# Listing the norms ahead of the merges, and the first weights ahead of the last two operands, in an encoder layer on one core

## The chip, the cores and the metric

The kernel runs on one core of one Trainium2 chip. The metric is device time of one launch, in microseconds (us). The kernel before the change takes 3186.42 us, the median of three runs (3184.72 to 3188.18).

## The reference, cut to what matters

One layer of an encoder is computed for two request groups, a prompt of 512 tokens and a sample of 1024, with the same weights. The model width is 1024, the inner width of the feed-forward block 2816, and all arithmetic is to fp32 accuracy. For a group with rows x:

```
h = rmsnorm(x, norm_pre_mix)
q, k, v, z, xbc, dt, gates = split(h @ w_in)
att = rmsnorm(diff_attention(q, k, v)) @ w_proj_attn
ssm = rmsnorm(ssd_forward + ssd_backward, gated by z) @ w_proj_ssm
merged = sigmoid(gate_att) * att + sigmoid(gate_ssm) * ssm
x  = x + rmsnorm(merged @ w_out, norm_post_mix)
h2 = rmsnorm(x, norm_pre_ffn)
up = h2 @ w_gate_up
y  = x + rmsnorm((silu(up[:, :2816]) * up[:, 2816:]) @ w_down, norm_post_ffn)
```

The change concerns the lines from `merged` to `up`.

## The kernel before, in words

**Tiles and chunks.** The 1536 tokens are worked on as three chunks of 512: chunk 0 is the prompt, chunks 1 and 2 the sample. An fp32 operand is held as a high and a low part in a format that TensorE multiplies (`split`, lines L135 and L136: ScalarE copies the high part, VectorE subtracts it to get the low one; with "act_pool" GpSimd subtracts, L142). A product of two operands is three matmuls per block of 128 rows: high with high (L167), high with low (L168), low with high (L169).

**What sets the order.** The program is written against a tile framework. The Python code lists operations; at compile time a scheduler hands each engine its instructions in one fixed order, in which what is listed first has precedence, and what is listed later fills in where it is ready by the scheduler's own reckoning. Tiles are taken from pools by tags; a tag has a fixed number of slots, and these are handed out in the order of the listing, so that a tile listed later waits for the readers of the one that had its slot before. On the chip every engine goes through its instructions strictly in that order. All loads and stores are issued by SyncE (SP).

**Merge of a chunk** (`merge`, L895 to L914). Four weight panels of 256 columns give eight products of 24 matmuls, each 512 columns wide, into a PSUM tile with the tag "mm", which has six slots. For each product a gate tile is loaded (L905, tag "gt", two slots) and put through tanh on ScalarE (L906), and the part of the state-space branch is loaded (L907, tag "pt", one slot). VectorE then empties the PSUM tile into the gate tile (L910), adds the part (L911), ScalarE writes the high part of the merged block (L912) and VectorE the low one (L913). Merge 0 is done earlier in another way; merge 1 and merge 2 are the ones here.

**Output projection of a chunk** (`out_proj`, L1040). Four panels of `w_out` by four tiles of 128 tokens give 16 PSUM tiles, also with the tag "mm", of 24 matmuls with 256 columns each, 384 matmuls in all. The sum runs over the eight merged blocks, so each of the 16 tiles needs all eight of them. ScalarE copies a PSUM tile to the rows `mt` (L1048) and squares it into a scratch tile of the tag "gt" for the sum of squares (L1050).

**Norms of a chunk** (`norms`, L1053 to L1081). VectorE sums the squares (L1057) and computes the reciprocal root by a short iteration of small instructions (L181 to L186). Then, for eight half rows of 512: the input is loaded (L1065, tag "xr", two slots), the row is scaled (L1066), the input is added (L1067), and ScalarE squares the sum (L1068); a finished row tile is stored (L1069). After a second reciprocal root the four row tiles are scaled (L1074), TensorE transposes them in 32 pieces, four to a PSUM tile (L1078), ScalarE copies each PSUM tile out with the weight of the norm (L1080) into a tile `hr` that takes the tags "gt" and "xr" in turn, and the result is stored for the feed-forward block (L1081).

**Gate-up.** The feed-forward product uses seven products in place of eight on 2 x 2 blocks. The first half of the tokens (768, from chunks 0 and 1) comes first; its operands are built by `Operands`: b11, t2, t3 and t1 by `build_first`, then b21, t4 and b22 by `build`. t4 is computed from b21 and t2; b22 is loaded and split. The sixth and seventh product of each step use t4 and b22. `weights(jb)` (L964) loads the weights of step jb (L974, four loads), forms sums on GpSimd (L989 to L997) and splits the seven results; `gate_up` (L1016) does the seven products of 12 matmuls with 384 columns, and empties them on ScalarE and VectorE (L1021 to L1033). Two steps (NPRE) stand in this part of the program, ahead of the norms of chunk 2; the others follow.

**The listing around the change** is at the end of the code below: the output projection of chunk 0, merge 1, norms of chunk 0, output projection 1, merge 2, norms of chunk 1, the operands, output projection 2, t4, b22, the weights of two steps, the two steps, norms of chunk 2.

Of the kernel before, what the change touches and what calls it, by code (L numbers as in the profile page):

```python
# [41 lines left out]
NPRE = 2  # L42
CB = (1, 1)
RWB = 7
NW = 0
NKEEP = 1
SEQS = ((0, 4), (4, 12))
GROUPS = ((0, 512), (512, 1024))
# [29 lines left out]
def hybrid_trunk_kernel(ctx: ExitStack, tc: tile.TileContext, a: dict, y_prompt, y_sample):  # L78
    nc = tc.nc
    V, S, G, TE = nc.vector, nc.scalar, nc.gpsimd, nc.tensor  # L80
# [3 lines left out]
    def f(ap):  # L84
        return ap.bitcast(F32)
# [273 lines left out]
    with ExitStack() as ph1:  # L359
# [230 lines left out]
        with tc.tile_pool(name="dp", bufs=1, reuse_waits="tile") as dp, tc.tile_pool(name="dp_ps", bufs=2, space=PSUM) as dps:  # L590
# [6 lines left out]
            t1 = dp.tile([P, NT, 32], F32, name="t1")  # L597
# [274 lines left out]
    with ExitStack() as ph3:  # L872
# [22 lines left out]
        def merge(c, aTt):  # L895
            cs = slice(c * 512, (c + 1) * 512)
            hi, lo = big_pair()
            for p0 in range(0, D, 256):
                w = split_panel(a["w_proj_attn"][0][:, p0:p0 + 256])
                for b in range(2):  # L900
                    r0 = p0 + b * P
                    kb = r0 // P
                    gt = wk.tile([P, 512], F32, tag="gt", name="gt")
                    pt = wk.tile([P, 512], F32, tag="pt", name="pt", bufs=1)
                    load(out=gt, in_=g_d[r0:r0 + P, cs])  # L905
                    S.activation(out=gt, in_=gt, func=AF.Tanh, scale=0.5)  # L906
                    load(out=pt, in_=part_d[r0:r0 + P, cs])  # L907
                    ps = mm_tile(512)
                    gemm_fm(ps, w, slice(b * P, (b + 1) * P), aTt)
                    V.scalar_tensor_tensor(gt, gt, 1.0, ps, op0=ALU.add, op1=ALU.mult)  # L910
                    V.tensor_add(gt, gt, pt)  # L911
                    S.activation(out=hi[:, kb, :], in_=gt, func=AF.Copy, scale=0.5)  # L912
                    V.scalar_tensor_tensor(lo[:, kb, :], gt, 0.5, f(hi[:, kb, :]), op0=ALU.mult, op1=ALU.subtract)  # L913
            return hi, lo  # L914
# [101 lines left out]
        def gate_up(t0, jb, ops, w, pool, bufs, tables=True):  # L1016
            c11, c12, c22 = [pool.tile([P, 384], F32, tag=t_, name=t_, bufs=b_)
                             for t_, b_ in (("c11", bufs), ("c12", bufs), ("c22", min(bufs, CB[1])))]
            c21 = wk.tile([P, 384], F32, tag="araw", name="c21", bufs=3) if bufs == 1 else pool.tile(
                [P, 384], F32, tag="c21", name="c21", bufs=CB[0])  # L1020
            S.copy(c11, product(w[0], ops[0]))  # L1021
            V.tensor_add(c12, product(w[1], ops[1]), c11)
            V.tensor_add(c21, product(w[2], ops[2]), c12)
            ps = product(w[3], ops[3])
            V.tensor_add(c22, ps, c21)
            V.tensor_add(c12, ps, c12)
            V.tensor_add(c11, product(w[4], ops[4]), c11)
            V.tensor_add(c21, product(w[5], ops[5]), c21)
            silu_mul(c11, c21, tables)
            store(out=ff_d[t0 // 768][jb * P:(jb + 1) * P, 0:384], in_=c11)  # L1030
            V.tensor_add(c12, product(w[6], ops[6]), c12)
            silu_mul(c12, c22, tables)
            store(out=ff_d[t0 // 768][jb * P:(jb + 1) * P, 384:768], in_=c12)  # L1033

        with ExitStack() as ph3a:
            mp = ph3a.enter_context(tc.tile_pool(name="mp", bufs=1, reuse_waits="tile"))
            pmw = mp.tile([P, D], F32, name="pmw")
            load(out=pmw, in_=a["norm_post_mix"].broadcast_to([P, D]))

            def out_proj(mT):  # L1040
                tiles = [mp.tile([P, D], F32, tag="mt", name="mt", bufs=4) for _ in range(4)]
                sums = wk.tile([P, 4, 4], F32, tag="ms4", name="ms4")
                for p0 in range(0, D, 256):
                    w = split_panel(a["w_out"][0][:, p0:p0 + 256])
                    for j in range(4):
                        ps = mm_tile(256)
                        gemm_tm(ps, w, mT, slice(j * P, (j + 1) * P))
                        S.copy(tiles[j][:, p0:p0 + 256], ps)  # L1048
                        sq = wk.tile([P, 256], F32, tag="gt", name="msq")
                        S.activation(out=sq, in_=ps, func=AF.Square, accum_out=sums[:, j, p0 // 256:p0 // 256 + 1])  # L1050
                return tiles, sums

            def norms(c, arg):  # L1053
                tiles, sums = arg
                v, r, t_ = [wk.tile([P, 2, 4], F32, tag=n, name=n) for n in ("mv", "mr", "mt_")]
                s2 = wk.tile([P, 4, 2], F32, tag="ms2", name="ms2")
                V.reduce_sum(v[:, 0], sums, axis=mybir.AxisListType.X)  # L1057
                V.tensor_scalar(v[:, 0], v[:, 0], 1.0 / D, EPS, op0=ALU.mult, op1=ALU.add)
                rsqrt(r[:, 0], v[:, 0], t_[:, 0])
                for j, mt in enumerate(tiles):  # L1060
                    t = 4 * c + j
                    for o in (0, 512):
                        mo = mt[:, o:o + 512]
                        xt = mp.tile([P, 512], F32, tag="xr", name="xr", bufs=2)
                        load(out=xt, in_=rows(t, a["x_prompt"], a["x_sample"])[:, o:o + 512])  # L1065
                        V.scalar_tensor_tensor(mo, mo, r[:, 0, j:j + 1], pmw[:, o:o + 512], op0=ALU.mult, op1=ALU.mult)  # L1066
                        V.tensor_add(mo, mo, xt)  # L1067
                        S.activation(out=xt, in_=mo, func=AF.Square, accum_out=s2[:, j, o // 512:o // 512 + 1])  # L1068
                    store(out=x2_d[t * P:(t + 1) * P, :], in_=mt)  # L1069
                V.tensor_add(v[:, 1], s2[:, :, 0], s2[:, :, 1])  # L1070
                V.tensor_scalar(v[:, 1], v[:, 1], 1.0 / D, EPS, op0=ALU.mult, op1=ALU.add)
                rsqrt(r[:, 1], v[:, 1], t_[:, 1])
                for j, mt in enumerate(tiles):
                    V.tensor_scalar(mt, mt, r[:, 1, j:j + 1], 0.0, op0=ALU.mult, op1=ALU.add)  # L1074
                for k in range(KB):
                    ps = tr_ps.tile([P, 512], F32, tag="tr", name="tr_ps")
                    for j, xn in enumerate(tiles):
                        TE.transpose(ps[:, j * P:(j + 1) * P], xn[:, k * P:(k + 1) * P], ident)  # L1078
                    hr = (mp if k % 2 else wk).tile([P, 512], F32, tag=("gt", "xr")[k % 2], name="hr", bufs=2)
                    S.activation(out=hr, in_=ps, func=AF.Copy, scale=cols[:, C_FFN + k:C_FFN + k + 1])  # L1080
                    store(out=h2_d[k * P:(k + 1) * P, c * 512:(c + 1) * 512], in_=hr)  # L1081

            def att(c):
                return load_att(c, big_pair(), lambda: [
                    wk.tile([P, 512], F32, tag="araw", name="araw", bufs=3) for _ in range(2)])

            m0 = load_merged(0)
            att_scale(1, zq, msq, ap, tr_ps, "tr")
            aT1 = att(1)
            t0 = out_proj(m0)  # L1090
            m1 = merge(1, aT1)
            norms(0, t0)
            aT2 = att(2)
            t1 = out_proj(m1)
            m2 = merge(2, aT2)
            norms(1, t1)
            ops = Operands(0, wk, "araw", 3)
            ops.build_first()
            ops.build(("b21",), V, "act_dve")
            t2 = out_proj(m2)  # L1100
            ops.build(("t4",), V, "act_dve")
            ops.tag, ops.bufs = OT
            ops.build(("b22",), V, "act_pool")
            w = {jb: weights(jb, "pt", 1) for jb in range(NPRE + NW)}
            for jb in range(NPRE):
                gate_up(0, jb, ops.all(), w[jb], mp, 1, False)
            norms(2, t2)

        with tc.tile_pool(name="fw", bufs=2, reuse_waits="tile") as fw:
            for jb in range(NPRE, FB):  # L1110
                if jb >= NPRE + NW:
                    w[jb] = weights(jb, rpool=fw if jb > NPRE else None)
                gate_up(0, jb, ops.all(), w[jb], fw, 2)
            ops = Operands(768, fw, "rw", RWB)
            ops.build_first()
            ops.build(ops.names[4:], G, "act_dve")
            for jb in reversed(range(FB)):
                if jb < FB - NKEEP:
                    w[jb] = weights(jb, rpool=fw)
                gate_up(768, jb, ops.all(), w[jb], fw, 2)  # L1120
# [104 lines left out]
```

## Time and profile before

| what | value |
|---|---|
| median of three runs | 3186.42 us |
| the profiled execution | 3193.28 us, span of the trace 3191.5 us |
| TensorE (PE) busy | 3035.2 us, 95% of the span |
| VectorE (DVE), ScalarE (ACT), GpSimd (POOL) busy | 57%, 39%, 20% of the span |
| mean granted TensorE clock | 0.98 of full speed |
| merge 1 begins on PE | 1893.17 us after the span's start |
| merge 2 begins | 2004.23 us |
| gate-up begins | 2100.14 us |

A row of a timeline or a group gives engine, line, operation, the tile written and those read, and sizes; what stands in brackets is the idle time of the engine just ahead, and what ended it. PEld is TensorE's loading of weights, which runs beside its matmuls; SPq and the like are an engine's queue of DMA issues. The clock is that which was granted to TensorE.

### The profile page before, as it was taken

What the parts mean: (1) busy time and instruction counts of PE and PEld (TensorE: products, weight loads), DVE (VectorE), ACT (ScalarE), POOL (GpSimd) and SP (SyncE); (2) the same over time, 40 slices, a digit from 0 to 9 for tenths busy, and PEclk for the clock granted to TensorE, in tenths of its full rate; (3) what the DMA queues carried; (4) which work ended last, traced back from release to release, by engine and by line L of the source; (5) the groups of instructions that cost most, each with busy time, mean ns of one, the idle gap of its engine ahead of it and who ended that gap; (6) DMA issues with size and microseconds to landing.
All of it is one profiled execution on the core that took longest, in us unless ns stands there. A gap on an engine that the chain in (4) does not pass through costs nothing. (4 is left out here: it accounts for less than half of the span.)

```text
span 3191.5 us, 44134 instructions
## 1 busy us (share of the span) xinstructions
PE 3035.2 (95%) x16667; PEld 2672.3 (84%) x16667; DVE 1826.8 (57%) x2957; ACT 1260.0 (39%) x2305; POOL 650.7 (20%) x508
## 2 busy tenths in 40 slices
PE   7999999999999999899999898978999999989998
PEld 7988887888787777788877787878999899978887
DVE  5214444455327996387778845676666766632444
ACT  4103333333303333366666645543333333332443
POOL 0001111000133442243232100023333433300000
PEclk9999999999999999999999999989999999999999
DMA  4633333223554445755546047644333333363454
GB/s 149 195 99 112 110 105 108 59 77 106 156 166 139 146 143 150 213 174 165 168 135 186 27 139 240 214 145 130 98 103 101 100 98 100 108 202 97 125 163 132
DMA packets 441341, 429.44 MB, mean 135 GB/s; under 512 B 25200, under 2 KB 358481, under 8 KB 440017
## 3 DMA queue, kind: packets, MB, share of 16 engines
q1 hardware_dynamic: 441129, 426.63, 43.2%
q8 instruction: 131, 2.15, 0.3%
q14 instruction: 81, 0.66, 0.1%
HBM read 314.48 MB, written 120.44 MB: 136 GB/s over the span
## 5 line engine op out<-in xcount | busy, mean ns | idle before, releaser
L167 PE MATMUL acc<-hT,whi 128*128 128x512 f32 x1056 | 421.6, 399 | 3.4 <-ACT st L453 3.4
L168 PE MATMUL acc<-hT,whi 128*128 128x512 f32 x1056 | 417.1, 395 | 0.0
L169 PE MATMUL acc<-hT,wlo 128*128 128x512 f32 x672 | 262.5, 391 | 0.0
L167 PEld LDWEIGHTS acc<-hT,whi 128*128 128x128 f32 x1056 | 199.1, 189 | 49.1 <-issue 5.8
L299 ACT ACTIVATE pt<-pt,nm 128x1024 f32<-128x1024 f32 (+1 forms) x192 | 193.1, 1006 | 111.3 <-DVE nm L296 108.0
L168 PEld LDWEIGHTS acc<-hT,whi 128*128 128x128 f32 x1056 | 199.2, 189 | 42.6 <-issue 3.6
L296 DVE CUSTOM_DVE_ANT_0 pt<-s,tb 128x1024 f32<-128x1024 f32 (+1 forms) x192 | 197.5, 1040 | 53.0 <-PE s L294 41.0
L167 PE MATMUL acc<-whi,hT 128*128 128x256 f32 x768 | 224.9, 293 | 1.2 <-ACT hT L206 0.6
L169 PE MATMUL acc<-whi,hT 128*128 128x256 f32 x768 | 225.1, 294 | 0.4 <-DVE hT L207 0.3
L168 PE MATMUL acc<-wlo,hT 128*128 128x256 f32 x768 | 223.3, 291 | 0.0
L167 PE MATMUL d<-dhi,fh 128*128 128x512 f32 x528 | 207.1, 392 | 5.9 <-ACT fh L135 5.9
L169 PE MATMUL d<-dhi,fl 128*128 128x512 f32 x528 | 206.8, 392 | 4.2 <-DVE fl L136 4.2
L168 PE MATMUL d<-dlo,fh 128*128 128x512 f32 x528 | 206.8, 392 | 0.0
L135 ACT CAST whi<-wraw 128x1024 fp32r<-128x1024 f32 (+1 forms) x115 | 115.9, 1036 | 214.0 <-PE acc L169 82.9
L136 DVE TENSOR_TENSOR fl<-raw,fh 128x896 fp32r<-128x896 f32 (+1 forms) x70 | 79.5, 1137 | 193.7 <-ACT fh L135 193.7
L167 PE MATMUL mm<-op,wy 128*128 128x384 f32 x528 | 178.9, 339 | 8.6 <-ACT op L135 6.9
L234 POOL TENSOR_TENSOR ql<-raw,qh 128x512 fp32r<-128x512 f32 x48 | 64.7, 1362 | 575.0 <-ACT qh L231 575.0
L169 PE MATMUL mm<-op,wy 128*128 128x384 f32 x528 | 178.7, 339 | 0.0
L168 PE MATMUL mm<-op,wy 128*128 128x384 f32 x528 | 178.4, 338 | 0.0
L136 DVE TENSOR_TENSOR wlo<-wraw,whi 128x1024 fp32r<-128x1024 f32 x80 | 95.4, 1221 | 112.9 <-ACT whi L135 103.5
L167 PEld LDWEIGHTS acc<-whi,hT 128*128 128x128 f32 x768 | 147.9, 193 | 11.7 <-issue 9.6
L169 PE MATMUL acc<-hT,whi 128*128 128x512 f32 x384 | 156.3, 407 | 0.0
(356 smaller groups left out, 8200.5 us busy)
## 6 DMA issues: line engine op xcount, KB each, us to landing
wraw<-in_w_in_dram SPq DMA_DIRECT2D x60, 512.0 KB
wraw<-in_w_gate_up_dram SPq DMA_DIRECT2D x92, 256.0 KB
raw<-ff_d SPq DMA_DIRECT2D x46, 448.0 KB
wr<-in_w_gate_up_dram SPq DMA_DIRECT2D x80, 256.0 KB
ff_d<-c SPq DMA_DIRECT2D x88, 192.0 KB
g_d<-st SPq DMA_DIRECT2D x48, 256.0 KB
xg<-xs_d SPq DMA_DIRECT2D x48, 256.0 KB
gt<-g_d SPq DMA_DIRECT2D x48, 256.0 KB
```

What stands on the lines that cost most here:

```text
L135: S.copy(hi, raw)
L136: V.tensor_sub(lo, raw, f(hi))
L167: TE.matmul(ps, ah, bh, start=(i == 0), stop=False)
L168: TE.matmul(ps, ah, bl, start=False, stop=False)
L169: TE.matmul(ps, al, bh, start=False, stop=(i == n - 1))
L234: G.tensor_sub(q_l[:, s_], q_r[:, s_], f(q_h[:, s_]))
L296: V.tensor_tensor_reduce(out=pt[:], in0=sps[:], in1=tb[:, off:off + SL], scale=-1.0, scalar=3.0e38, op0=ALU.add, op1=ALU.min, accum_out=nm ...
L299: S.activation(out=pt, in_=pt, func=AF.Exp, bias=nm[:, m:m + 1], scale=-1.0, accum_out=(z0, zs[:, 0:1])[m])
```

## The change

No operation is added or taken away. The listing is changed in three places. The norms of chunks 0 and 1 are each listed right behind the output projection that they belong to, and so ahead of merge 1 and merge 2; before, they stood behind these merges. The weights of the first gate-up step are listed ahead of the operands t4 and b22, and those of the second step behind the first step. And the low part of b22 is computed by VectorE, where GpSimd did it. The rest of the diff takes out a constant that was 0.

```diff
-NW = 0
...
             t0 = out_proj(m0)
+            norms(0, t0)
             m1 = merge(1, aT1)
-            norms(0, t0)
             aT2 = att(2)
             t1 = out_proj(m1)
+            norms(1, t1)
             m2 = merge(2, aT2)
-            norms(1, t1)
             ops = Operands(0, wk, "araw", 3)
             ops.build_first()
             ops.build(("b21",), V, "act_dve")
             t2 = out_proj(m2)
+            w = {0: weights(0, "pt", 1)}
             ops.build(("t4",), V, "act_dve")
             ops.tag, ops.bufs = OT
-            ops.build(("b22",), V, "act_pool")
-            w = {jb: weights(jb, "pt", 1) for jb in range(NPRE + NW)}
+            ops.build(("b22",), V, "act_dve")
             for jb in range(NPRE):
+                if jb:
+                    w[jb] = weights(jb, "pt", 1)
                 gate_up(0, jb, ops.all(), w[jb], mp, 1, False)
             norms(2, t2)
...
             for jb in range(NPRE, FB):
-                if jb >= NPRE + NW:
-                    w[jb] = weights(jb, rpool=fw if jb > NPRE else None)
+                w[jb] = weights(jb, rpool=fw if jb > NPRE else None)
                 gate_up(0, jb, ops.all(), w[jb], fw, 2)
```

The instructions of each engine show what the scheduler makes of it. Line numbers in the changed kernel are one lower from L45 on, since a line is gone: its L909 is L910 before, its L1077 is L1078. First VectorE where merge 1 meets the norms of chunk 0; `mt` are the rows being normed, `gt` the gate tile, `mm` the PSUM tile of a merge product. Before:

```order
L910 SCALAR_TENSOR_TENSOR gt<-gt,mm 128x512
L185 SCALAR_TENSOR_TENSOR mt__17030<-mt__17030,mv 128x4
L911 TENSOR_TENSOR gt<-gt,pt 128x512
L186 SCALAR_TENSOR_TENSOR mr<-mt__17030,mr 128x4
L1066 SCALAR_TENSOR_TENSOR mt<-mt,mr,pmw 128x512 x8
L913 SCALAR_TENSOR_TENSOR big<-gt,big 128x512
L1067 TENSOR_TENSOR mt<-mt,xr 128x512
L136 TENSOR_TENSOR big<-araw,big 128x512
L1067 TENSOR_TENSOR mt<-mt,xr 128x512
L136 TENSOR_TENSOR big<-araw,big 128x512
L910 SCALAR_TENSOR_TENSOR gt<-gt,mm 128x512
```

And in the change, where all eight additions of the inputs stand further ahead:

```order
L184 SCALAR_TENSOR_TENSOR mt__16716<-mt__16716,mv 128x4
L185 SCALAR_TENSOR_TENSOR mr<-mt__16716,mr 128x4
L1073 TENSOR_SCALAR mt<-mt,mr 128x1024 x4
L909 SCALAR_TENSOR_TENSOR gt<-gt,mm 128x512
L910 TENSOR_TENSOR gt<-gt,pt 128x512
L909 SCALAR_TENSOR_TENSOR gt<-gt,mm 128x512
L912 SCALAR_TENSOR_TENSOR big<-gt,big 128x512
```

Before, the emptyings of the merge stand between the steps of the norms. Now the first of them stands behind the last scaling of the norms. TensorE has the transposes of chunk 0 in one piece, behind 144 rows of merge 1 (six products); before they stood four at a time within output projection 1:

```order
L166 MATMUL mm<-big,whi 128x512
L167 MATMUL mm<-big,whi 128x512
L168 MATMUL mm<-big,wlo 128x512
L1077 MATMUL tr_ps<-ident,mt 128x128 x32
L166 MATMUL mm<-big,whi 128x512
L167 MATMUL mm<-big,whi 128x512
L168 MATMUL mm<-big,wlo 128x512
```

Second, SP's loads and stores in merge 1. `g_d` and `part_d` hold the gates and the parts, `h_d` the normed rows, `x_d` the sums of input and mixer. Before:

```order
L351 DMA araw<-r_d_82 128x512
L349 DMA araw<-att_d 128x512
L905 DMA gt<-g_d 128x512 x2
L154 DMA wraw<-in_w_proj_attn_dram 128x4x256 x2
L907 DMA pt<-part_d 128x512
L905 DMA gt<-g_d 128x512
L351 DMA araw<-r_d_82 128x512
L1065 DMA xr<-in_x_prompt_dram 128x512
L1069 DMA x_d<-mt 128x1024
L1065 DMA xr<-in_x_prompt_dram 128x512
```

In the change:

```order
L1068 DMA x_d<-mt 128x1024
L153 DMA wraw<-in_w_out_dram 128x4x256 x2
L1080 DMA h_d<-hr 128x512 x7
L904 DMA gt<-g_d 128x512
L1080 DMA h_d<-hr 128x512
L1064 DMA xr<-in_x_sample_dram 128x512
L904 DMA gt<-g_d 128x512
L1064 DMA xr<-in_x_sample_dram 128x512
L906 DMA pt<-part_d 128x512
L904 DMA gt<-g_d 128x512
L350 DMA araw<-r_d_82 128x512
L906 DMA pt<-part_d 128x512
```

The first gate load has moved behind seven of the eight stores of the norms, and the first part load behind all of them.

Third, VectorE at the start of gate-up. Before, the norms of chunk 2 begin ahead of the first emptying of the first step (L1022); `s`, `wraw` are weights being split, `c` the results of a step:

```order
L186 SCALAR_TENSOR_TENSOR mr<-mt__19093,mr 128x4
L1066 SCALAR_TENSOR_TENSOR mt<-mt,mr,pmw 128x512 x8
L136 TENSOR_TENSOR wlo<-s_18813,wlo 128x512
L1067 TENSOR_TENSOR mt<-mt,xr 128x512 x2
L136 TENSOR_TENSOR whi<-wraw,whi 128x512
L1022 TENSOR_TENSOR c_18866<-mm,c_18865 128x384
```

In the change:

```order
L185 SCALAR_TENSOR_TENSOR mr<-mt__19093,mr 128x4
L1027 TENSOR_TENSOR c_18836<-mm,c_18836 128x384
L135 TENSOR_TENSOR whi<-wraw,whi 128x512
L135 TENSOR_TENSOR wy<-wraw,wy 128x512
L1065 SCALAR_TENSOR_TENSOR mt<-mt,mr,pmw 128x512 x7
L1013 SCALAR_TENSOR_TENSOR c_18833<-c_18833,c_18836 128x384
L1065 SCALAR_TENSOR_TENSOR mt<-mt,mr,pmw 128x512
L1030 TENSOR_TENSOR c_18834<-mm,c_18834 128x384
```

The first step's emptyings up to that of the sixth product (L1027, L1028 before) now stand ahead of the norms' scaling.

## The prediction

> **What bounds the kernel now.** I read the page first, then the busy time by stage, then the timelines of the engines in the stage that the diff touches.
>
> ```profile
> PE 3035.2 (95%) x16667; PEld 2672.3 (84%) x16667; DVE 1826.8 (57%) x2957; ACT 1260.0 (39%) x2305; POOL 650.7 (20%) x508
> 1890.00:1943.00 53.00, 49.15 (x222) 40.43 (x222) 41.17 (x68) 28.54 (x58) 0.00 (x0) 0.97 0.76 258
> 1943.00:2004.00 61.00, 53.17 (x415) 51.60 (x414) 23.98 (x41) 29.90 (x71) 0.00 (x0) 0.94 0.57 183
> 2004.00:2048.00 44.00, 44.00 (x198) 36.52 (x197) 34.08 (x68) 21.35 (x39) 0.00 (x0) 1.00 0.72 235
> 2048.00:2100.00 52.00, 49.98 (x415) 49.24 (x414) 30.06 (x48) 31.37 (x80) 0.00 (x0) 1.00 0.55 179
> 2100.00:2175.00 75.00, 43.19 (x217) 38.33 (x216) 59.15 (x106) 30.29 (x66) 25.06 (x15) 0.80 0.42 137
> ```
>
> After the window's length the columns are PE, PEld, DVE, ACT and POOL busy, then the clock, the DMA share and GB/s. PE is the bound, at 95%. The rows are merge 1, output projection 1, merge 2, output projection 2, and the first gate-up steps. In the first four PE idles 13.7 us in 210; in the last 31.8 of 75. There is little to win in the merges and up to 32 us behind them.
>
> ```profile
> 1893.17 0.40 PE L167 MATMUL mm<-big,whi 128*128 128x512 f32 x1
> 2004.23 0.40 PE L167 MATMUL mm<-big,whi 128*128 128x512 f32 x1
> 2100.14 0.34 PE L167 MATMUL mm<-op,whi 128*128 128x384 f32 x1
> 2117.96 0.69 PE L167 MATMUL mm<-op,whi 128*128 128x384 f32 x1 [15.57 <-ACT whi L135]
> 2163.45 2.58 PE L1078 MATMUL tr_ps<-ident,mt 128*128 128x128 f32 x8 [7.68 <-DVE mt L1074]
> ```
>
> These are marks on PE: merge 1 begins at 1893.17, merge 2 at 2004.23, gate-up at 2100.14. So stage 1 (merge and projection) takes 111.1 us and stage 2 95.9. The gate-up holes are 15.57 us for the first weights and 7.68 us for norms(2).
>
> **The change part by part.** Lines are those of the kernel before; in the change's order rows they stand one lower. No arithmetic is added; only order changes, and four POOL subtractions go to DVE.
>
> Part one, norms(0) ahead of merge 1 and norms(1) ahead of merge 2. The order now has all 32 transposes behind the sixth merge product, and the first L910, which empties the first product's PSUM tile, behind the last L1074. There are six such tiles. The seventh product therefore waits for the norms, the transposes, and then a gate load, because the gate tile shares its two slots with the rows that norms stores last. The queues show the same: on SP eight input loads, four x2 stores and seven of eight h2 stores now stand ahead of the first gate load, and behind that the part loads; on ACT the first tanh stands behind the eight copies out of the transposes. What is late next is the merged operand: eight emptyings that ran beside eight products now run one after another, and the projection behind them needs all eight. Products seven and eight and the first 138 matmuls of the projection fit between the emptyings (10.9 and 16.6 us of work in 37) and cost nothing.
>
> The norms' chain before, on DVE:
>
> ```profile
> 1903.85 0.16 DVE L1057 TENSOR_REDUCE mv<-ms 128x4 f32<-128x16 f32 x1
> 1909.55 5.39 DVE L1066 SCALAR_TENSOR_TENSOR mt<-mt,mr,pmw 128x512 f32<-128x512 f32 x8
> 1915.45 0.69 DVE L1067 TENSOR_TENSOR mt<-mt,xr 128x512 f32<-128x512 f32 x1
> 1940.16 0.68 DVE L1067 TENSOR_TENSOR mt<-mt,xr 128x512 f32<-128x512 f32 x1
> 1952.58 1.41 DVE L1074 TENSOR_SCALAR mt<-mt,mr 128x1024 f32<-128x1024 f32 x2
> 2005.21 0.17 DVE L1057 TENSOR_REDUCE mv<-ms 128x4 f32<-128x16 f32 x1 [8.22 <-ACT msq L1050]
> 2017.39 0.68 DVE L1067 TENSOR_TENSOR mt<-mt,xr 128x512 f32<-128x512 f32 x1
> 2019.18 0.73 ACT xr L1068 x2
> 2027.10 5.17 DMA xr<-in_x_sample_dram
> 2040.15 0.69 DVE L1067 TENSOR_TENSOR mt<-mt,xr 128x512 f32<-128x512 f32 x1
> L136 DVE TENSOR_TENSOR wlo<-wraw,whi 128x1024 fp32r<-128x1024 f32 x32 | 38.4, 1221 | 32.5 <-ACT whi L135 32.5
> ```
>
> It starts 10.7 us into stage 1 and 1.0 us into stage 2. (1) From L1057 to the first L1067 11.1 us pass without L913; 1.3 of them are the L910 and L911 that now go: 9.8. (2) Eight L1067 on two input slots are three rounds of load, add, square: 5.17 + 0.69 + 0.73 = 6.6, so 19.8 (before 24.7 and 22.8, from first to seventh L1067). (3) Seventh and eighth L1067 1.3, square 0.73, a dozen small rows at 0.2, two weight splits 2.4, four L1074 at about 0.7: 9.8. The sum is 39.4. The first squares also wait 1 to 2 us behind four weight casts on ACT. The chain thus ends 51 us into stage 1 and 42 into stage 2. Merge products start 5.44 us apart:
>
> ```profile
> 1905.35 0.39 PE L167 MATMUL mm<-big,whi 128*128 128x512 f32 x1
> 1910.79 0.39 PE L167 MATMUL mm<-big,whi 128*128 128x512 f32 x1
> 2170.43 1.24 PE L1078 MATMUL tr_ps<-ident,mt 128*128 128x128 f32 x8 [0.35 <-ACT hr L1080]
> 1904.33 0.90 SPq L905 DMA_DIRECT2D gt<-g_d  x2
> 1907.36 0.63 ACT L906 ACTIVATE gt<-gt 128x512 f32<-128x512 f32 x1 [4.50 <-DMA gt<-g_d]
> 2033.61 5.19 DMA gt<-g_d
> ```
>
> So PE is through six products after 33 to 38 us and stands. Then the 32 transposes in a row: norms(2) shows them, 2163.45 to 2171.67, 8.2 us. Then a gate load: between 3.03 (1904.33 to 1907.36) and 5.19, I take 4.1, the middle; with tanh 0.63, L910 and L911 at 0.69 each and 0.8 of issue and hand-over, 6.9. Then seven more emptyings. Their cycle goes by the single pt slot: each load is issued as the L911 before it ends.
>
> ```profile
> 1920.73 0.69 DVE L911 TENSOR_TENSOR gt<-gt,pt 128x512 f32<-128x512 f32 x1
> 1956.10 0.69 DVE L911 TENSOR_TENSOR gt<-gt,pt 128x512 f32<-128x512 f32 x1 [0.84 <-DMA pt<-part_d]
> 1960.67 0.69 DVE L911 TENSOR_TENSOR gt<-gt,pt 128x512 f32<-128x512 f32 x1
> 2044.34 5.70 DMA pt<-part_d
> 1960.39 0.28 PE L168 MATMUL mm<-wlo,big 128*128 128x256 f32 x1
> 1960.51 0.28 PE L169 MATMUL mm<-whi,big 128*128 128x256 f32 x1
> ```
>
> Six cycles from 1920.73 to 1960.67 mean 6.66 us; the shortest, the last, is 4.57. The queue is emptier now, since the norms' loads and stores are done, so I take 5.3, nearer the short end: 37.1 for seven. L912 and L913 add 1.4. In the change's order 246 of the projection's 384 matmuls stand behind the first that needs the eighth block; at 0.12 us that is 29.5. Six tiles that end together and the clock's ramp take 3.0:
>
> ```profile
> 1972.99 0.58 PE L167 MATMUL mm<-whi,big 128*128 128x256 f32 x1 [3.79 <-ACT msq L1050]
> 1977.86 0.42 PE L168 MATMUL mm<-wlo,big 128*128 128x256 f32 x1
> 1978.07 0.41 PE L169 MATMUL mm<-whi,big 128*128 128x256 f32 x1
> ```
>
> After that hole the matmuls still come 0.21 us apart 5.1 us later, where 0.12 is the full pace: 5.1 x (1 - 0.12 / 0.21) = 2.2 us lost. The other 0.8 I set for the tiles.
>
> Stage 1: 51 + 8.2 + 6.9 + 37.1 + 1.4 + 29.5 + 3.0 = 137.1, against 111.1: **+26.0**. Stage 2: 42 and the same, 128.1, against 95.9: **+32.2**.
>
> The Trainium skill, TensorE: Matmul & The Clock Gate, section "Part 1: The HAM clock gate", says that about 3.4 us of idling halves the clock and that as long a busy window restores it. The rows agree on the half rate but show 5.1 us of it. By the rule a ramp costs half of 3.4, 1.7 and not 2.2, an estimate; the sum would be 1 us less. It also speaks against the change: between two emptyings PE would run cold.
>
> Part two, weights(0) ahead of t4 and b22, and b22's low part on DVE. Four weights(0) loads and their casts, which stood behind t4 and b22, now stand among the projection's last emptyings on ACT and DVE, so the 15.57 us hole should close; t4 and b22 are first needed by the sixth and seventh product, 9 us and more into the step, which hides them. But PE then waits for norms(2), whose order is what counts:
>
> ```profile
> 2123.55 7.46 DVE L1066 SCALAR_TENSOR_TENSOR mt<-mt,mr,pmw 128x512 f32<-128x512 f32 x8
> 2162.55 2.74 DVE L1074 TENSOR_SCALAR mt<-mt,mr 128x1024 f32<-128x1024 f32 x4
> ```
>
> L1066 began 23.4 us after 2100.14, and 41.7 us later L1074 ended. In the change L1066 stands behind L1028 of the first step, which takes the sixth product: 72 matmuls of 384 columns, by the 256-wide ones 0.12 x 1.5 = 0.18 us each, 13.0, and a split, about 13.5. So the chain and the transposes move up by **10** us (bounds 5 and 18: a stretch of splits ahead of L1066, or fewer rows inside the 41.7). The hole does not vanish; most of it moves ahead of the transposes. The four b22 subtractions that DVE takes over (384 wide, so under the 0.69 of a 512-wide L911) are hidden beside the first six products; uncovered they would cost up to 2.8.
>
> Sum: 26.0 + 32.2 - 10 = **+48.2**. The profiled execution took 3193.28 (span 3191.5), so it becomes 3241.5; the median of the runs, 3186.42, becomes 3234.6, that is **3235**.
>
> **Rivals.** A, the loads stay as slow as now: cycle 6.66 gives +1.36 x 14 = 19, rounds of 24.7 and 22.8 give 8, together 3262. For it: 5.70, 5.17 and 5.19 are waits on the chain. Against: DMA share was 0.76 and 0.72 there with the norms mixed in. B, no gain at gate-up, because a weight slot frees late: 3245. C, calm loads: with all at 3.03, rounds lose 6.4, the gate 1.1, the cycles 10.3 per stage, 35.6 in all: 3199. D, the other side: load time decides, 11 loads in a row per stage, so 22 us per us of load. From 2.8 us on, and with the full 18 at gate-up, nothing is lost; at 2.6 the time is 3182. Against it: the shortest gate load that an engine waited for is 3.03, and two to four loads fly at once. The Trainium skill, DMA: Bandwidth & Descriptors, section "Anatomy of one DMA — SWDGE (gpsimd) path", fits 2.0 us plus size over 436 GB/s for POOL's issue path, 2.6 us for these 256 KB, an estimate; SP's rows here are longer.
>
> **How the numbers follow.** The forecast 0.55, A 0.17, B 0.13, C 0.10, D 0.05. Range 3198 to 3264: C to just over A. A change of 0.2%, 6.4 us, can be told from none in this kernel. Only D is not slower, and some room is left that C goes further: faster 0.04, same 0.03, slower 0.93.
>
> **What would show it.** On PE, two holes of 9 to 18 us ahead of 32 transposes, naming L1074, then waits on L910 to L913; L911 rows about 5.3 us apart, all behind the transposes; stages of about 137 and 128 us; the first gate-up product within 3 us of the projection, and a hole of some 15 us ahead of the third set of transposes. Wrong if L910 rows stand between the L1067, if L911 rows come under 3.5 us apart, or if the stages last under 115 and 100.

## The result, and the profile after

The changed kernel takes 3216.03 us, the median of six runs (3213.21 to 3225.99); the kernel before took 3185.10 us beside it (six runs, 3181.36 to 3188.18). The ratio is 1.0097, 95% interval 1.0082 to 1.0112: **slower by 31 us**. Forecast were 48 us, 3235 in a range of 3198 to 3264. The profiled execution took 3221.56 us, with a span of 3219.7. PE is still the bound by the page's first part, with the same matmuls and 12 us more of busy time, at a mean granted clock of 0.978 where it was 0.980:

```profile
PE 3047.3 (95%) x16667; PEld 2673.2 (83%) x16667; DVE 1833.2 (57%) x2961; ACT 1259.4 (39%) x2305; POOL 645.0 (20%) x504
```

The marks on TensorE, from its timeline, as the prediction showed them of before: merge 1 begins, its transposes, the first merge product behind them; merge 2 begins, its transposes, the first merge product behind them; gate-up begins, the third transposes.

```profile
1887.53 0.40 PE L166 MATMUL mm<-big,whi 128*128 128x512 f32 x1
1934.07 2.67 PE L1077 MATMUL tr_ps<-ident,mt 128*128 128x128 f32 x8 [13.39 <-DVE mt L1073]
1947.76 0.79 PE L166 MATMUL mm<-big,whi 128*128 128x512 f32 x1 [5.05 <-DVE gt L909]
2019.36 0.40 PE L166 MATMUL mm<-big,whi 128*128 128x512 f32 x1
2057.46 2.59 PE L1077 MATMUL tr_ps<-ident,mt 128*128 128x128 f32 x8 [5.26 <-DVE mt L1073]
2072.03 0.79 PE L166 MATMUL mm<-big,whi 128*128 128x512 f32 x1 [6.01 <-DVE gt L909]
2136.94 0.34 PE L166 MATMUL mm<-op,whi 128*128 128x384 f32 x1
2188.51 2.59 PE L1077 MATMUL tr_ps<-ident,mt 128*128 128x128 f32 x8 [11.18 <-DVE mt L1073]
2191.66 5.86 PE L1077 MATMUL tr_ps<-ident,mt 128*128 128x128 f32 x24 [0.56 <-ACT hr L1079]
```

Stage 1 now lasts 2019.36 - 1887.53 = 131.8 us (before 111.1), stage 2 117.6 (before 95.9). From gate-up's begin to the end of the third transposes it is 2197.52 - 2136.94 = 60.6, where it was 71.5. So 20.7 + 21.7 - 10.9 = 31.5 us, which is the measured difference. Both losses are where the prediction put them: PE stands ahead of each block of 32 transposes for L1073 (before L1074), then for the first emptying (L909, before L910), in stage 1 for 13.39 and 5.05 us and in stage 2 for 5.26 and 6.01. The 15.57 us hole behind gate-up's first matmuls is gone, and 11.18 us of waiting stand ahead of the third transposes.

The busy time by window shows what became of the merges. The columns are the window's length, PE, PEld, DVE, ACT and POOL busy, the clock, the DMA share and GB/s. The rows are the wait and transposes of stage 1, its emptyings, the projection behind them, and the same two windows of stage 2.

```profile
1920.70:1942.70 22.00, 8.06 (x32) 5.29 (x32) 9.41 (x22) 8.49 (x15) 0.00 (x0) 0.61 0.65 226
1942.70:1987.00 44.30, 31.75 (x168) 28.16 (x168) 27.24 (x40) 17.06 (x28) 0.00 (x0) 0.85 0.68 214
1987.00:2019.40 32.40, 32.16 (x268) 31.96 (x268) 7.26 (x6) 16.33 (x51) 0.00 (x0) 1.00 0.33 105
2052.00:2066.00 14.00, 8.06 (x33) 5.14 (x32) 6.92 (x19) 6.00 (x8) 0.00 (x0) 0.63 0.58 196
2066.00:2105.60 39.60, 29.63 (x179) 26.07 (x179) 27.43 (x47) 18.40 (x32) 0.00 (x0) 0.91 0.65 202
```

PE is idle for 14 of 22 us, and then for 13 of 44 while the emptyings run one by one; the projection's rest is full work again. VectorE's rows of each stage: the last scalings of the norms, the first emptying of stage 1, and the first and last part addition (L910, before L911):

```profile
1933.26 2.74 DVE L1073 TENSOR_SCALAR mt<-mt,mr 128x1024 f32<-128x1024 f32 x4
1947.02 0.69 DVE L909 SCALAR_TENSOR_TENSOR gt<-gt,mm 128x512 f32<-128x512 f32 x1 [11.02 <-ACT gt L905]
1947.74 0.69 DVE L910 TENSOR_TENSOR gt<-gt,pt 128x512 f32<-128x512 f32 x1
1984.89 0.69 DVE L910 TENSOR_TENSOR gt<-gt,pt 128x512 f32<-128x512 f32 x1
2056.55 2.74 DVE L1073 TENSOR_SCALAR mt<-mt,mr 128x1024 f32<-128x1024 f32 x4
2072.36 0.68 DVE L910 TENSOR_TENSOR gt<-gt,pt 128x512 f32<-128x512 f32 x1
2103.34 0.69 DVE L910 TENSOR_TENSOR gt<-gt,pt 128x512 f32<-128x512 f32 x1
```

All sixteen part additions stand behind their norms: seven cycles of 5.31 us in stage 1 and of 4.43 in stage 2.

### The profile page after: what moved, and what is told of

Its sections match the earlier page's. It is cut to its first block, busy times and chain, and to the rows that moved or that the text cites. A ratio compares the mean times of both kernels' runs of the same rounds, so it can differ in the third digit from the quotient of the medians.

```text
span 3219.7 us, 44129 instructions
## 1 busy us (share of the span) xinstructions
PE 3047.3 (95%) x16667; PEld 2673.2 (83%) x16667; DVE 1833.2 (57%) x2961; ACT 1259.4 (39%) x2305; POOL 645.0 (20%) x504
## 4 chain that ended last, share of the span: by engine, by line
PE 61%; DMA 15%; DVE 9%; issue 5%; ACT 5%; POOL 3%; SPq 1%; ACTq 0%; POOLq 0%; DVEq 0%
PE acc L166 9%; PE acc L168 9%; PE acc L167 9%; PE mm L166 4%; PE mm L167 4%; PE mm L168 4%; PE d L168 4%; PE d L167 4%; PE d L166 3%; DMA wraw<-in_w_gate_up_dram 2%; DMA araw<-r_d 2%; DMA gt<-g_d 2%; DMA raw<-k_d 1%; DVE pt L295 1%; PE s L292 1%
## 5 line engine op out<-in xcount | busy, mean ns | idle before, releaser
L135 DVE TENSOR_TENSOR wlo<-wraw,whi 128x1024 fp32r<-128x1024 f32 x80 | 96.2, 1230 | 103.0 <-ACT whi L134 92.5
```

Of the source, the lines that this page charges most:

```text
L135: V.tensor_sub(lo, raw, f(hi))
```

## The experiments

Twelve kernels. The table gives the ratio to the kernel before, run beside each, and the two stages and gate-up (to the end of the third transposes) from the profile of each. Executions differ by some 6 us either way ahead of these stages (merge 1 began between 1886.9 and 1898.7 us), so places are compared by stage, not by totals. Where the third transposes stand behind more products, the last column doesn't compare and is left out.

| kernel | ratio (interval) | stage 1 | stage 2 | gate-up |
|---|---|---|---|---|
| before | 1 | 111.1 | 95.9 | 71.5 |
| the change | 1.0097 (1.0082 to 1.0112) | 131.8 | 117.6 | 60.6 |
| norms_only | 1.0106 (1.0091 to 1.0121) | 128.8 | 119.0 | 64.3 |
| weights_only | 1.0013 (0.9998 to 1.0027) | 111.5 | 95.6 | 73.3 |
| norms0_only | 1.0084 (1.0063 to 1.0104) | 129.8 | 95.5 | 72.7 |
| norms1_only | 1.0080 (1.0061 to 1.0099) | 110.9 | 118.7 | 65.2 |
| norms1_weights | 1.0031 (1.0016 to 1.0046) | 112.4 | 118.6 | 61.3 |
| hr_other_slot | 0.9990 (0.9981 to 1.0000) | 105.0 | 95.7 | |
| two_pt | 1.0114 (1.0099 to 1.0129) | 129.1 | 115.6 | 61.2 |
| no_att2 | one profile | 121.0 | 119.6 | 60.9 |
| hr_other_slot_npre3 | 1.0004 (0.9992 to 1.0016) | 105.1 | 95.6 | |
| before_hr_slot | 0.9995 (0.9982 to 1.0008) | 107.9 | 95.9 | |
| before_hr_slot_4xr | 0.9978 (0.9967 to 0.9990) | 107.7 | 95.8 | |
| hr_other_slot_4xr | 0.9983 (0.9970 to 0.9997) | 104.8 | 96.0 | |

### Each part alone

norms_only, on the kernel before, moves both norms and leaves the rest:

```diff
+            norms(0, t0)
             m1 = merge(1, aT1)
-            norms(0, t0)
...
+            norms(1, t1)
             m2 = merge(2, aT2)
-            norms(1, t1)
```

> The norms of chunks 0 and 1 ahead of the merges; weights, t4 and b22 as before. Theory (the loss is all in the two merge stages, the gain all in the weights' place): the two stages lose 42 us as in the change (20.7 and 21.7) and nothing is won at gate-up, 3185 + 42 = 3227 us (3221 to 3233), and the hole of some 15 us before the first gate-up product is back. Rival (the gain at gate-up came from the norms of chunk 1 being done earlier): 3216 us, the same as the change, with no such hole.

weights_only is the rest of the change, with the norms where they were:

```diff
             t2 = out_proj(m2)
+            w = {0: weights(0, "pt", 1)}
             ops.build(("t4",), V, "act_dve")
...
-            ops.build(("b22",), V, "act_pool")
-            w = {jb: weights(jb, "pt", 1) for jb in range(NPRE + NW)}
+            ops.build(("b22",), V, "act_dve")
             for jb in range(NPRE):
+                if jb:
+                    w[jb] = weights(jb, "pt", 1)
...
```

> The listing of weights, t4 and b22 as in the change, the norms as before. Theory: merge stages of 111 and 96 us as before, and gate-up up to the third transposes 11 us shorter, 3185 - 11 = 3174 us (3169 to 3179). Rival (the gain needs the earlier norms): 3185 us, no change.

The theory failed in both. The norms alone already win 7 us at gate-up, and the weights' place alone wins nothing (73.3 in place of 71.5, ratio 1.0013). In the timeline of PE the hole at gate-up's first weights shrinks under either part, first norms_only, then weights_only:

```profile
2151.99 0.69 PE L167 MATMUL mm<-op,whi 128*128 128x384 f32 x1 [6.33 <-ACT whi L135]
...
2103.49 0.69 PE L166 MATMUL mm<-op,whi 128*128 128x384 f32 x1 [7.32 <-ACT whi L134]
```

It was 15.57. With the weights alone, what the first gate-up step wins is lost again in the second: the first lasts 24.7 us in place of 36.2, the second 28.6 in place of 17.1, with a hole of 5.19 us ahead of its seventh product. L1073 starts 63.8 us into gate-up, L1074 before started at 62.4. With the norms alone it starts at 54.4.

What the norms do at gate-up shows in the stores of chunk 1's rows (SP) and the casts of the operands that are loaded from them (ACT). First the kernel before (the first and the last row of the eight stores, and the cast), then the change:

```profile
2055.54 0.50 SPq L1081 DMA_DIRECT2D h_d<-hr  x1
2072.45 0.46 SPq L1081 DMA_DIRECT2D h_d<-hr  x1
2072.39 0.57 ACT L135 CAST op<-rw 128x384 fp32r<-128x384 f32 x1
```

```profile
2060.58 0.92 SPq L1080 DMA_DIRECT2D h_d<-hr  x2
2067.88 0.41 SPq L1080 DMA_DIRECT2D h_d<-hr  x1
2074.62 1.32 ACT L134 CAST op<-rw 128x384 fp32r<-128x384 f32 x3
```

Gate-up begins at 2100.14 before and at 2136.94 after. So these casts begin some 28 us ahead of it before and some 62 us ahead now (before, a single cast of b11, which needs chunk 0 alone, stands at 2011.94). In the 20 us ahead of gate-up PE is full in both; in the 15 us behind its begin PE is busy for 2.25 us before and for all 15 now.

### One chunk's norms at a time

Each is one of norms_only's two moves alone: norms1_only that of chunk 1, norms0_only that of chunk 0.

> Only the norms of chunk 1 go ahead of merge 2; all else as before. Theory now (what is won at gate-up comes from chunk 1 being normed and stored earlier, since the operands are built from it): stage 2 loses 22 to 23 us, and gate-up up to the first product of its fourth step gains 9, so 13 to 14 us over before, about 3199 us on a base of 3185 (3195 to 3204). Rival (the gain belongs to the place of the weights): no gain, 22 us over before, 3207 us.

> Only the norms of chunk 0 go ahead of merge 1; all else as before. Theory now: stage 1 loses 18 to 21 us, stage 2 and gate-up stay, so 18 to 21 us over before, about 3204 us on a base of 3185 (3200 to 3209). Rival (the norms of chunk 0 carry a part of the gain at gate-up): 3195 us or less.

The stages come out as the theory said: each move costs its own stage, 22.8 and 18.7 us, and leaves the other alone. Gate-up is 6.3 us shorter with chunk 1's norms and not with chunk 0's (72.7). The times are further from before than that: 25 and 27 us by the ratios, where stages and gate-up give 16.3 and 19.5, with intervals of 6 to 7 us either way. Where the rest lies is open.

norms1_weights adds the rest of the change to norms1_only:

> The change without the move of chunk 0's norms: chunk 1's norms ahead of merge 2, and the new place of the weights, t4 and b22. Theory (the hole at the first gate-up weights closes only if the operands are built early, which chunk 1's norms allow, and the weights stand ahead, which the other part does): no such hole, gate-up up to the first product of its fourth step 11 us shorter as in the change, stage 2 22 us longer, 11 us over before in all. Rival (chunk 0's norms carry the rest): gate-up 7 us shorter or less, with a hole of 5 us or more, 15 us over before or more.

It holds: gate-up takes 61.3 us, 10.2 less than before, its first matmuls run on without a hole, and the ratio of 1.0031 is 10 us (5 to 15). So chunk 1's norms build the operands early, the weights' place uses that, and only both together close the hole; chunk 0's norms have no part in it.

### What puts the emptyings behind the norms

hr_other_slot is the change with one line altered: the transposed rows no longer take gate slots. They have two slots then, where they had four.

```diff
-                    hr = (mp if k % 2 else wk).tile([P, 512], F32, tag=("gt", "xr")[k % 2], name="hr", bufs=2)
+                    hr = mp.tile([P, 512], F32, tag="xr", name="hr", bufs=2)
```

> The change as it is, with its listing; only the eight tiles hr, which carry the transposed rows to their stores, all take the tag xr, and none takes gt any more, so that the gate tiles of the merge no longer wait for the norms' last stores. Theory (the shared gt slots put the emptyings behind the norms): emptyings between the steps of the norms as before, no hole ahead of 32 transposes, stages near 111 and 96 us, 3174 us (3169 to 3181), since the gain at gate-up stays. Rival (the norms' chain itself, listed first, takes VectorE ahead of the merge): above 3205 us, near the change's 3216.

The theory holds in the merges. VectorE works on merge products (L910 adds the part behind an emptying) between the additions of the inputs (L1066) again, with the listing of the change:

```profile
1907.30 0.69 DVE L910 TENSOR_TENSOR gt<-gt,pt 128x512 f32<-128x512 f32 x1
1914.01 0.69 DVE L1066 TENSOR_TENSOR mt<-mt,xr 128x512 f32<-128x512 f32 x1
...
1948.53 0.68 DVE L910 TENSOR_TENSOR gt<-gt,pt 128x512 f32<-128x512 f32 x1
1949.32 1.42 DVE L1073 TENSOR_SCALAR mt<-mt,mr 128x1024 f32<-128x1024 f32 x2
```

Both losses are gone, 105.0 and 95.7 us. The listing as such costs nothing in these stages: the gate tiles, which take their slots behind the norms' last stores, did it. The 11 us at gate-up are gone as well, since chunk 1's norms are no earlier than before (the casts that need them begin 29.5 us ahead of gate-up): from gate-up's begin to the first product of its fourth step it is 87.0 us, before 87.1, in the change 75.4. And the fewer slots have a price. ACT's copies of the third transposes wait four times, 6.3 us in all, for a store of hr, waits that are not there before; the longest:

```profile
2172.36 0.69 ACT L1079 ACTIVATE hr<-tr_ps,cols 128x512 f32<-128x512 f32 x1 [1.92 <-DMA h_d<-hr]
```

The first product of the fifth step comes 107.0 us into gate-up, before 101.8; in before_hr_slot (below), where this line alone differs from before, it comes at 105.8. So the whole is only 3 us under before, an interval that ends at no difference.

### What sets the cycle of the emptyings

The prediction let the single slot of the part tile set it. two_pt gives every second part tile another slot:

```diff
-                    pt = wk.tile([P, 512], F32, tag="pt", name="pt", bufs=1)
+                    pt = mp.tile([P, 512], F32, tag="c11", name="pt", bufs=1) if b else wk.tile([P, 512], F32, tag="pt", name="pt", bufs=1)
```

> The change with a second slot for the part tile of the merge (every second one takes the tag c11). Theory (the emptyings' cycle goes by the one pt slot): then the two gate slots set it. A gate slot goes round in load 3.0 + tanh 0.63 + four steps of 0.6 to 0.7 + some 1.2 of hand-over = 7.5 us for two products, 3.8 each in place of 5.3 and 4.4, so 7 x 1.5 + 7 x 0.6 = 15 us less than the change, 3201 us (3196 to 3208). Rival (the gate slots, or VectorE's own order, set the cycle already): 3213 to 3217 us.

The theory fell: the cycles are 4.8 and 4.1 us long in place of 5.3 and 4.4, where 3.8 was expected, the stages are 2.7 and 2.0 us shorter, and the whole isn't faster than the change. The groups of VectorE in the change between 1920 and 1990 us show why. Behind the last bar stands the idle time ahead of each group and what ended it:

```profile
L910 DVE TENSOR_TENSOR gt<-gt,pt 128x512 f32<-128x512 f32 x8 | 5.5, 689 | 2.6 <-DMA pt<-part_d 2.4
L909 DVE SCALAR_TENSOR_TENSOR gt<-gt,mm 128x512 f32<-128x512 f32 x8 | 5.5, 686 | 13.8 <-ACT gt L905 13.7
L351 DVE SCALAR_TENSOR_TENSOR araw<-araw,cols 128x512 f32<-128x512 f32 x6 | 4.5, 751 | 6.3 <-DMA araw<-r_d 6.3
```

Only 2.4 us are waits for a part. Of L909's 13.7 us, 11.02 belong to the first emptying, as its row above has it. The largest wait between emptyings, 6.3 us, is L351: these rows prepare chunk 2's attention operand, stand between the emptyings in VectorE's fixed order and each wait for their own load. no_att2 takes them away:

```diff
-            aT2 = att(2)
...
-            m2 = merge(2, aT2)
+            m2 = merge(2, aT1)
```

> The change without the loads, scaling and splits of chunk 2's attention operand, which stand among the emptyings of merge 1 (merge 2 takes chunk 1's operand again, so a part of the result is left out of the computation). Theory (those rows, in VectorE's fixed order and each waiting for its own load, stretch the emptyings): the seven cycles of the emptyings of merge 1 take 29 us or less in place of 37, at 4.2 each, and stage 1 about 124 us in place of 132. Rival (the gate and part loads alone set the cycle, the other rows fill their waits): 5.3 each and 132 us as in the change.

```profile
1952.52 0.69 DVE L910 TENSOR_TENSOR gt<-gt,pt 128x512 f32<-128x512 f32 x1
1956.18 0.69 DVE L910 TENSOR_TENSOR gt<-gt,pt 128x512 f32<-128x512 f32 x1 [0.49 <-DMA pt<-part_d]
1982.21 0.69 DVE L910 TENSOR_TENSOR gt<-gt,pt 128x512 f32<-128x512 f32 x1
```

The seven cycles take 29.7 us in place of 37.2, which the theory had as 29. Stage 1 is 121.0 us, 10.8 less; the other 3 us come ahead of the transposes, which begin 43.2 us into the stage in place of 46.5. Whether it is the waits of these rows, their work or their loads that stretched the cycles, this run doesn't tell apart. What is left, 4.2 us, has no run of its own; in this trace the emptyings behind the first still wait 8.5 us for a gate's tanh, and the additions 2.7 us for a part.

### Trying for more

hr_other_slot_npre3 changes hr_other_slot's NPRE from 2 to 3:

> The change with hr on the tag xr alone, and with three gate-up steps in place of two ahead of the norms of chunk 2. Theory (TensorE has nothing to do while those norms end: a hole of 8 to 11 us ahead of their transposes in three of the runs): the third step fills it, 5 to 8 us under the same kernel with two steps, some 3178 us on a base of 3186. Rival (the third step's weights and results wait for the slots of the first two, so that the hole only moves): no gain, about 3185 us.

No gain (1.0004): the rival holds as to time. The theory had taken its hole from other kernels: in hr_other_slot the third transposes follow a gate-up product at once (2162.35, no idle time ahead), so there was none to fill. To the first product of the sixth step it is 119.4 us in place of 121.7, which the time doesn't show. before_hr_slot puts hr_other_slot's line into the kernel before:

> The kernel before, with hr on the tag xr alone. Theory (the shared gt slots cost something in the old listing too: the hole of 3.8 us behind the transposes, where the projection's scratch tile waits for a store of hr): stage 1 at 105 us in place of 111, 5 to 6 us under before. Rival (the shorter stage 1 came from the new listing): 111 us, no difference.

Undecided: stage 1 is 107.9 us, between the two, and the time can't be told from before. The wait of the scratch tile for a store of hr (0.86 us ahead of L1050 on ACT) is gone, but the copies into hr, with two slots in place of four, wait up to 3.26 us for such a store, and of the hole of 3.79 us 2.45 are left. before_hr_slot_4xr and hr_other_slot_4xr add input slots in the norms of chunk 2, on the one kernel and the other:

```diff
-                        xt = mp.tile([P, 512], F32, tag="xr", name="xr", bufs=2)
+                        xt = (wk if c == 2 and j % 2 else mp).tile([P, 512], F32, tag="gt" if c == 2 and j % 2 else "xr", name="xr", bufs=2)
```

> The same, and in the norms of chunk 2 half of the inputs are loaded into the gt slots, so that four loads can fly in place of two. Theory (the rounds of two loads make the third norms late, and TensorE waits for these): the eight additions take 12 us in place of 20, the hole of 8 us ahead of the third transposes goes, 6 to 8 us under the kernel with two slots. Rival (VectorE's queue, full of weight splits there, sets the pace): no difference from two slots.

> The change with hr on the tag xr alone and with the four input slots in the norms of chunk 2. Theory (as with the kernel before): 6 to 8 us under the change with hr on xr alone, which was 3 us under before, so about 10 us under before. Rival (VectorE's queue sets the pace): 3 us under before, no difference from two slots.

The first and the last additions (L1067) of chunk 2's norms, of the eight, and the scaling behind them, in before_hr_slot and then in before_hr_slot_4xr:

```profile
2129.25 1.28 DVE L1067 TENSOR_TENSOR mt<-mt,xr 128x512 f32<-128x512 f32 x2
2150.84 0.69 DVE L1067 TENSOR_TENSOR mt<-mt,xr 128x512 f32<-128x512 f32 x1 [1.17 <-DMA xr<-in_x_sample_dram]
2162.70 2.74 DVE L1074 TENSOR_SCALAR mt<-mt,mr 128x1024 f32<-128x1024 f32 x4
```

```profile
2134.80 1.88 DVE L1067 TENSOR_TENSOR mt<-mt,xr 128x512 f32<-128x512 f32 x3
2146.66 0.68 DVE L1067 TENSOR_TENSOR mt<-mt,xr 128x512 f32<-128x512 f32 x1
2163.35 3.53 DVE L1074 TENSOR_SCALAR mt<-mt,mr 128x1024 f32<-128x1024 f32 x4
```

From the first to the last it is 11.9 us in place of 21.6, as expected. But gate-up begins at 2097.54 in the one and 2102.15 in the other, so L1074 starts only 4.0 us earlier in it (61.2 us in place of 65.2), behind gate-up's emptyings and splits of weights in VectorE's queue: part theory, part rival. A hole of 8 us ahead of the third transposes was not there to go: it is missing in both kernels with two slots. To the first product of gate-up's fifth step the four slots win 3.0 us on the kernel before (102.8 in place of 105.8) and 4.0 on the change (103.0 in place of 107.0), where 6 to 8 were expected. At 0.9978 (0.9967 to 0.9990), before_hr_slot_4xr has the lowest ratio of all, 7 us under before and 38 under the change; hr_other_slot_4xr, at 0.9983, can't be told from it, nor from hr_other_slot.

## Why the prediction was right, and where its steps were not

The direction, the two places and the mechanism of the loss were right, and 48 us was half as much again as the 31.5 in the trace. The terms, measured in the same way:

| term of the sum | forecast, stage 1 / 2 | measured, stage 1 / 2 |
|---|---|---|
| the norms' chain ends, into the stage | 51 / 42 | 48.5 / 39.9 |
| transposes | 8.2 / 8.2 | 6.7 / 6.7 |
| gate load to the end of the first part addition | 6.9 / 6.9 | 5.7 / 7.0 |
| seven cycles of emptyings | 37.1 / 37.1 | 37.2 / 31.0 |
| the rest of merge and projection | 33.9 / 33.9 | 33.8 / 32.9 |
| stage | 137.1 / 128.1 | 131.8 / 117.6 |

**The emptyings were over-sized in stage 2**, the largest single miss, 6.1 us. The step that failed is that their cycle goes by the pt slot, with one length for both stages. In stage 1 the length came out to the tenth by luck, for another reason: the attention rows in VectorE's queue, without which it is 4.2. No attention rows stand in merge 2, and its 4.43 is near that.

**The chain and the transposes** were 2 to 2.5 and 1.5 us too long. The transposes themselves took 8.6 us in each stage, but they began under the last L1073 (1934.07, with L1073 running to 1936.00), and the sum had them one after the other; the table counts them from the end of L1073.

**The rest came out right by luck too.** The sum lets the projection wait for the eighth block, then run 246 matmuls and lose 2.2 us to the clock. In stage 1 TensorE last stood for the sixth block (L912); its product began at 1979.36, and from there it was never idle for more than 0.3 us. The eighth block was done at 1986.97, and some 267 matmuls still ran behind that, at a granted clock of 1.00. So the last two emptyings were hidden.

```profile
1978.61 0.68 DVE L912 SCALAR_TENSOR_TENSOR big<-gt,big 128x512 fp32r<-128x512 f32 x1
1979.36 0.95 PE L168 MATMUL mm<-whi,big 128*128 128x256 f32 x3 [1.97 <-DVE big L912]
1986.28 0.69 DVE L912 SCALAR_TENSOR_TENSOR big<-gt,big 128x512 fp32r<-128x512 f32 x1 [0.70 <-ACT big L911]
```

**The gain at gate-up was right in size and wrong in cause.** 10 were forecast, 10.9 came. The prediction gave all of it to part two, where the first steps' weights move. The runs give that part alone no gain, chunk 1's norms alone 6.3, and both 10.2. What was overlooked is that norming chunk 1 early also lets the operands be built early: the cost was worked out for every reader of the gate slots, and nobody asked who reads the norms' result. The size was luck: the working had the scaling of chunk 2's norms (L1065, before L1066) begin 13.5 us into gate-up and let the rows from there to the end of L1073 last 41.7 us as before. It began at 19.9, and they lasted 33.5.

```profile
2156.87 3.39 DVE L1065 SCALAR_TENSOR_TENSOR mt<-mt,mr,pmw 128x512 f32<-128x512 f32 x5
2187.61 2.74 DVE L1073 TENSOR_SCALAR mt<-mt,mr 128x1024 f32<-128x1024 f32 x4
```

**The rivals.** A (loads as slow as before) had cycles of 6.66 us, C (calm loads) of 5.3 - 10.3 / 7 = 3.8; 5.31 and 4.43 lie between them, nearer C in stage 2. B (no gain at gate-up) is what weights_only shows, but the change has the gain. D, that it might not be slower, needed loads of 2.8 us, 0.2 less than C's, so cycles of about 3.6 us, and 18 us at gate-up; neither came.

**The signs.** L910 rows behind the transposes, 5.3 us apart in stage 1, the holes that name L1073, and gate-up's first products without a hole all stood as foretold; of the holes 13.39 us in stage 1 lies within what was said, 5.26 in stage 2 and 11.18 at gate-up are less. The stages of 137 and 128 did not, but stayed clear of the 115 and 100 that would have refuted them.

## What to carry to other kernels

Where slots are handed out in the order of the listing, moving a block ahead moves it in every queue that shares a tag with it: ask of each tag which tiles behind the moved block now wait for its last readers. Here a single shared tag turned a harmless move into 42 us, and taking it away undid them. And a moved producer must be costed from both ends, by what it delays and by who can start on its result earlier.

## What the runs showed of the hardware

The clock around the holes of stage 1. The columns are those of the windows above, with the clock third from the end. The rows are the last of the transposes and what follows, the end of the 5.05 us hole, the merge products behind it, and those behind these.

```profile
1942.00:1945.00 3.00, 0.72 (x6) 0.42 (x4) 0.00 (x0) 1.27 (x3) 0.00 (x0) 1.00 0.88 279
1945.50:1947.70 2.20, 0.00 (x0) 0.00 (x0) 0.68 (x1) 0.63 (x1) 0.00 (x0) 0.50 0.97 331
1947.70:1952.00 4.30, 4.24 (x10) 3.37 (x11) 2.98 (x6) 2.18 (x4) 0.00 (x0) 0.50 0.50 152
1952.50:1956.00 3.50, 3.50 (x17) 2.89 (x16) 2.11 (x4) 1.01 (x2) 0.00 (x0) 1.00 0.74 232
```

The clock fell to half in the hole of 13.39 us, came back within the transposes, at 1941.9, fell again at 1945.3, 2.6 us after the last transpose, and came back at 1952.1. So the merge products ran at half rate for 4.4 us, behind the second hole alone:

```profile
1951.77 0.57 PE L166 MATMUL mm<-big,whi 128*128 128x512 f32 x1
1952.18 0.39 PE L167 MATMUL mm<-big,whi 128*128 128x512 f32 x1
1952.41 0.39 PE L168 MATMUL mm<-big,wlo 128*128 128x512 f32 x1
```

They started 0.43 us apart from 1948.36 on, and 0.23 apart from 1952.18 on. That costs about half of the 4.4, some 2 us. In stage 2 the half rate lasted 3.0 us behind the hole of 6.01. The changes of the clock in the two stages, read in windows of 0.1 us (1924.9, 1941.9, 1945.3, 1952.1, then 2054.5, 2064.7, 2068.2, 2075.0), lie 3.4 us or near multiples of it apart within each stage, so how long the slow clock lasts seems to depend on where in such a period the work begins; no run tests that.

The Trainium skill (TensorE: Matmul & The Clock Gate, "Part 1: The HAM clock gate") asks for at least one busy window of about 3.4 us, which would lose 1.7, an estimate; the 4.4 us of stage 1 are longer than one, the 3.0 of stage 2 a little shorter. The clock fell 2.6 us after the last transpose, sooner than by the 3.4 us of idling that the prediction took from the same section. The holes themselves, 18.4 us in stage 1, cost far more than the slow clock behind them.
